# A hybrid encoder layer: the weight block sums of its FFN pairs on VectorE, and the norm factor behind one more unit

## The chip, the cores and the metric

The kernel runs on one core of a Trainium2 chip. Measured is the device time of one execution in microseconds (us); several runs are made, and their median is given. Engines are named as in the profile: PE is TensorE's matmul, PEld its weight load, DVE is VectorE, ACT is ScalarE, POOL is GpSimd, SP is the engine whose queue issues most DMAs.

## The reference

One layer of an encoder over 512 tokens of width 1024. Around every sub-layer stands an RMS norm; the first and the last sub-layer are SwiGLU feed-forward networks of width 2816, and between them stands a mixer of a recurrent branch and windowed attention.

```python
def swiglu(x, w1, w3, w2):
    return (jax.nn.silu(x @ w1) * (x @ w3)) @ w2

f = swiglu(rms_norm(h, ffn1_pre_g), ffn1_w1, ffn1_w3, ffn1_w2)
h = h + 0.5 * rms_norm(f, ffn1_post_g)
...                                   # recurrent branch and attention, merged by gates
f = swiglu(rms_norm(h, ffn2_pre_g), ffn2_w1, ffn2_w3, ffn2_w2)
h = h + 0.5 * rms_norm(f, ffn2_post_g)
```

Attention adds a bias looked up in a table of 32 buckets by 16 heads (`rel_bias`). All arrays are float32.

## The kernel before, in words

Every product is made from float32 operands that are split into a high part in fp32r and the remainder in fp32r: `hi` by an ACT copy, `lo` by a DVE subtraction (`split2`, lines 180 to 183; for weights `split_to`, lines 140 to 150). A product takes three matmuls: hi by hi, lo by hi, hi by lo.

A *unit* (`unit`, `mm_feat`, lines 185 to 202) makes one block of 128 output features for all 512 tokens: 8 steps of k times three matmuls, 24 matmuls of 512 columns, from one weight block of 128x1024. `get` hands out the next weight block and lets the following ones be loaded (`dma_to`, on SP's queue) and split (`split_to`) a fixed number of blocks ahead. The order of all weight blocks stands in the list `order`. Instructions run on each engine in the order in which the program emits them; nothing is rearranged. Work that belongs to a unit but is to be emitted later is put into a list by `later(n, fn)`, and `point()`, called twice in every unit and once in every product of a pair, emits what is due.

The first FFN begins with x in place of its norm: the norm's factor is one number a token, so it may be applied to the products. Three units (w1a 0, w3a 0, w1a 1) run as the loads arrive, then unit w3a 1 (line 643). Meanwhile ACT sums the squares of x (line 638), `rstd_of` makes the factor `r` (lines 215 to 230), and line 642 puts `r` on the diagonal of four 128x128 blocks (`dgs`). A float32 matmul of a block of ones with each of them (line 655) spreads the factor over all partitions; ACT copies it to `Rb`. In front of that a float32 matmul of the one-hot table with `rel_bias` (line 646) makes the row of biases for each head, which POOL's DMA queue writes out 128 times (`bias_scr`, 3 MB) for attention to read later. Then the first units are scaled with `Rb` and put through SiLU (`silu_mul`), x itself is scaled (`norm_x`, line 722) and cut into quarters for the pairs, while the units 2 to 5 of w1a and w3a run (`swiglu_units`).

The other blocks of the two FFNs are made in *pairs* (`class Pairs`): two weight blocks of one matrix, taken as a 2x2 matrix of blocks with the activations as another, are multiplied with seven products in place of eight, by sums of blocks. There are 16 such jobs in the first FFN and 18 in the second, w1 and w3 by turns. A product (`mm_s`) has 12 matmuls of 256 columns. `prep(m, i)` gets job m's weights ready:

- step 0 makes the four weight sums `S12` and `S34` on POOL (lines 478 to 481),
- steps 1 to 4 split the raw block, `S12`, `S34` and the block `a22`.

While job n runs, steps 1 to 4 of job n + 1 are emitted, at its end step 0 of job n + 2, and then the loads for job n + 3. In job n the order on PE is: a11, s1, then a22 of the job before (`last`), s2, a12, s4, s3; in the very last job a12 comes behind s3. The partial results are taken out of PSUM by ACT copies (`q1`, `q5`, `u`, `v`, lines 510 to 537) and DVE adds (lines 528, 533, 538). The bank `bu` holds a11, then a11 + s2, then s3 on top, then a22 on top: each product that is added must wait until the sum so far has been read. `tail` (`w2_ahead`) splits the first two hidden blocks and the first two blocks of w2 in the last job, for the product that follows (`tok_gemm`).

All tiles share 38 slots of 4 KB a partition, and all PSUM tiles 8 banks; a tile waits until the one that had its slot before has been read for the last time.

Of the kernel before, what the change touches and what calls it, by code (L numbers as in the profile page):

```python
# [15 lines left out]
P = 128  # L16
# [35 lines left out]
def hybrid_layer(ctx: ExitStack, tc: tile.TileContext, a: dict, out: bass.AP):  # L52
# [10 lines left out]
    def slot(shape, dt=F32, name="s"):  # L63
        uid[0] += 1
        return sb.tile(shape, dt, tag="slot", name=f"{name}_{uid[0]}")

    def bank(name="ps"):
        uid[0] += 1
        return pp.tile([P, 512], F32, tag="ps", name=f"{name}_{uid[0]}")
# [96 lines left out]
    def later(n, fn, rank=1):  # L166
        uid[0] += 1
        due.append((now[0] + n, rank, uid[0], fn))
# [29 lines left out]
    def unit(nm, i, **kw):  # L198
        w = get(nm, i)
        ps = bank("f")  # L200
        mm_feat(ps, w, **kw)
        return ps
# [185 lines left out]
    def silu_mul(ps1, ps3, R=None):  # L388

        t = slot([P, 2, SEQ], name="sw")  # L390
        if R is None:
            act.activation(t[:, 0, :], ps1, AF.Silu)
            dve.tensor_tensor(out=t[:, 1, :], in0=ps3, in1=t[:, 0, :], op=ALU.mult)
        else:
            dve.tensor_tensor(out=t[:, 0, :], in0=ps1, in1=R, op=ALU.mult)
            dve.tensor_tensor(out=t[:, 1, :], in0=ps3, in1=R, op=ALU.mult)
            act.activation(t[:, 0, :], t[:, 0, :], AF.Silu)
            dve.tensor_tensor(out=t[:, 1, :], in0=t[:, 1, :], in1=t[:, 0, :], op=ALU.mult)
        return t[:, 1, :]
# [40 lines left out]
    class Pairs:  # L440
# [13 lines left out]
        def prep(self, m, i):  # L454
            if m >= len(self.jobs):
                return
            k = self.k0 + 2 * m
            if i == 0:
                if k not in loaded or k + 1 not in loaded:
                    self.raws(m)  # L460
                s12, s34 = slot([P, 2 * QH], name="S12"), slot([P, 2 * QH], name="S34")
                self.w[m] = {"r": (raws.pop(k), raws.pop(k + 1)), "s": (s12, s34)}
            W = self.w[m]
            (ra, rb), (s12, s34) = W["r"], W["s"]
            a11, a12, a21, a22 = ra[:, :QH], ra[:, QH:], rb[:, :QH], rb[:, QH:]

            def both(src, w=2 * QH):
                hi = slot([P, w], F32R, name="whi")
                lo = slot([P, w], F32R, name="wlo")
                split2(hi, lo, src)  # L470
                return hi, lo

            def halves(p, a, b):
                W[a] = p[0][:, :QH], p[1][:, :QH]
                W[b] = p[0][:, QH:], p[1][:, QH:]

            if i == 0:
                pool.tensor_tensor(out=s12[:, :QH], in0=a21, in1=a22, op=ALU.add)
                pool.tensor_tensor(out=s12[:, QH:], in0=s12[:, :QH], in1=a11, op=ALU.subtract)
                pool.tensor_tensor(out=s34[:, QH:], in0=a12, in1=s12[:, QH:], op=ALU.subtract)  # L480
                pool.tensor_tensor(out=s34[:, :QH], in0=a11, in1=a21, op=ALU.subtract)
            elif i == 1:
                halves(both(ra), "a11", "a12")
            elif i == 2:
                halves(both(s12), "s1", "s2")
            elif i == 3:
                halves(both(s34), "s3", "s4")
            elif i == 4:
                t = slot([P, 2, QH], F32R, name="w22")
                split2(t[:, 0, :], t[:, 1, :], a22)  # L490
                W["a22"] = t[:, 0, :], t[:, 1, :]
                del W["r"], W["s"]

        def run(self, tail, hooks={}):
            X = self.X
            assert st["get"] == st["split"] == self.k0, (st, self.k0)
            st["get"] = st["split"] = self.k0 + 2 * len(self.jobs)
            last = lambda: None
            for n, (nm, f) in enumerate(self.jobs):
                W = self.w.pop(n)  # L500
                first = nm == self.na
                tmp = slot([P, 4, 256], name="ct")
                q1, q5, u, v = (tmp[:, i, :] for i in range(4))
                c = slot([P, 2, SEQ], name="cc")
                if first:
                    self.c1[f] = c
                bu, bx, bc = (bank("c")[:, :256] for _ in range(3))
                at = lambda i: [f() for f in hooks.get((n, i), ())]
                mm_s(W["a11"], X["b11"], bu)
                act.activation(q1, bu, AF.Copy)  # L510
                at(1)
                mm_s(W["s1"], X["t1"], bx)
                act.activation(q5, bx, AF.Copy)
                at(2)
                last()
                self.prep(n + 1, 1)
                mm_s(W["s2"], X["t2"], bu, True)
                del W["s1"], W["s2"]
                act.activation(u, bu, AF.Copy)
                at(3)  # L520
                if n == len(self.jobs) - 1:
                    tail()
                self.prep(n + 1, 2)

                def c11():
                    mm_s(W["a12"], X["b21"], bc)
                    del W["a11"], W["a12"]
                    dve.tensor_tensor(out=c[:, 0, :256], in0=bc, in1=q1, op=ALU.add)

                if n < len(self.jobs) - 1:  # L530
                    c11()
                mm_s(W["s4"], X["b22"], bx, True)
                dve.tensor_tensor(out=c[:, 0, 256:], in0=bx, in1=u, op=ALU.add)
                self.prep(n + 1, 3)
                mm_s(W["s3"], X["t3"], bu, True)
                del W["s3"], W["s4"]
                act.activation(v, bu, AF.Copy)
                dve.tensor_tensor(out=c[:, 1, 256:], in0=v, in1=q5, op=ALU.add)
                if n == len(self.jobs) - 1:
                    c11()  # L540
                if first:
                    act.activation(c[:, 0, :], c[:, 0, :], AF.Silu)
                    act.activation(c[:, 1, 256:], c[:, 1, 256:], AF.Silu)
                else:
                    c1 = self.c1[f]
                    dve.tensor_tensor(out=c1[:, 0, :], in0=c1[:, 0, :], in1=c[:, 0, :], op=ALU.mult)
                    dve.tensor_tensor(out=c1[:, 1, 256:], in0=c1[:, 1, 256:], in1=c[:, 1, 256:], op=ALU.mult)
                self.prep(n + 1, 4)
                self.prep(n + 2, 0)
                self.raws(n + 3)  # L550

                def last(W=W, bu=bu, c=c, f=f, first=first):
                    mm_s(W.pop("a22"), X["t4"], bu, True)
                    if first:
                        act.activation(c[:, 1, :256], bu, AF.Silu)
                    else:
                        c1 = self.c1.pop(f)
                        dve.tensor_tensor(out=c1[:, 1, :256], in0=bu, in1=c1[:, 1, :256], op=ALU.mult)
                        self.hid.f += [c1[:, 0, :], c1[:, 1, :]]

            last()
# [40 lines left out]
    dma_one(pairs_a.k0)  # L602
    dma_one(pairs_a.k0 + 1)
    make_identity(nc, ident)
    ones = slot([P, P], name="ones")
    pool.memset(ones, 1.0)
    oh = slot([N_BUCKETS, NREL + 1 + N_HEADS], name="oh")
    pool.dma_start(out=oh[:, : NREL + 1], in_=a["onehot"])
    pool.dma_start(out=oh[:, NREL + 1 :], in_=a["rel_bias"])
    ps = [bank("f") for _ in range(NS)]  # L610

    def split_first(u, kp):
# [24 lines left out]
        junk = slot([P, D], name="junk")  # L637
        act.activation(junk, h_all[:, t, :], AF.Square, accum_out=s4[:, t : t + 1])
    r = rstd_of(s4)
    dgs = slot([P, NT, P], name="dgs")  # L640
    for t in range(NT):
        dve.tensor_scalar(out=dgs[:, t, :], in0=ident, scalar1=r[:, t : t + 1], scalar2=None, op0=ALU.mult)
    ps.append(unit("w3a", 1))

    pse = bank("e")
    pe.matmul(pse[:N_HEADS, : NREL + 1], oh[:, NREL + 1 :], oh[:, : NREL + 1], start=True, stop=True)
    erow = slot([N_HEADS, NREL + 1], name="erow")
    act.activation(erow, pse[:N_HEADS, : NREL + 1], AF.Copy)
    scr = tc.dram_tile([N_HEADS, P, NREL], F32, name="bias_scr")
# [1 line left out]
    pool.dma_start(out=scr, in_=bass.AP(tensor=ev.tensor, offset=ev.offset, ap=[ev.ap[0], [0, P], ev.ap[1]]))  # L651
    Rb = slot([P, SEQ], name="Rb")
    psr = bank("r")
    for t in range(NT):
        pe.matmul(psr[:, t * P : (t + 1) * P], ones, dgs[:, t, :], start=True, stop=True)
    act.activation(Rb, psr, AF.Copy)
    pairs_a.prep(0, 1)
    pairs_a.prep(0, 2)
# [23 lines left out]
        dve.tensor_scalar(out=cneg, in0=z[3], scalar1=-4.0, scalar2=None, op0=ALU.mult)  # L682
        dve.tensor_scalar(out=bhalf, in0=vec[:, V_BA : V_BG + 16], scalar1=0.5, scalar2=None, op0=ALU.mult)

    def swiglu_units(na, nb, f0, f1, hid, R=None):
        for f in range(f0, f1):
            p1, p3 = unit(na, f), unit(nb, f)
            later(1, lambda p1=p1, p3=p3: hid.f.append(silu_mul(p1, p3, R)))

    def uview(hh, th):  # L690

# [40 lines left out]
    later(11, lambda: X1.update(t2=to_slots(tn[1])))  # L732
    end = 2 * 2 * (NC1 - 2)
    later(end - 1, lambda: pairs_a.prep(1, 0))
    swiglu_units("w1a", "w3a", 2, NC1, hid, Rb)
    point(True)
    X1["b21"] = to_uT(xn[1, 0], 1, 0)

# [441 lines left out]
```

## Time and profile before

| | us |
|---|---|
| median of 3 runs | 1155.74 |
| lowest, highest | 1155.67, 1157.07 |
| span of the profiled execution, first to last instruction | 1155.6 |
| PE busy in that span | 1138.0 |
| DVE busy | 779.9 |
| ACT busy | 574.3 |
| POOL busy | 353.0 |

The profile shows one execution of its own. Its page gives the span alone as the execution's time; the runs are timed from outside. A row of a timeline reads: start and length in us, engine, line of the kernel, operation, output and inputs, their shapes, how many were merged, and in brackets how long the engine had been idle before and what ended that. The second number in the row of a group is the mean in ns of one. Matmul rows overlap, since matmuls are pipelined: what counts there is the distance from start to start.

### The profile page before, as it was taken

What the parts mean: (1) busy time and instruction counts of PE and PEld (TensorE: products, weight loads), DVE (VectorE), ACT (ScalarE), POOL (GpSimd) and SP (SyncE); (2) the same over time, 40 slices, a digit from 0 to 9 for tenths busy, and PEclk for the clock granted to TensorE, in tenths of its full rate; (3) what the DMA queues carried; (4) which work ended last, traced back from release to release, by engine and by line L of the source; (5) the groups of instructions that cost most, each with busy time, mean ns of one, the idle gap of its engine ahead of it and who ended that gap; (6) DMA issues with size and microseconds to landing.
All of it is one profiled execution on the core that took longest, in us unless ns stands there. A gap on an engine that the chain in (4) does not pass through costs nothing.

```text
span 1155.6 us, 17108 instructions
## 1 busy us (share of the span) xinstructions
PE 1138.0 (98%) x6691; PEld 1011.8 (88%) x6691; DVE 779.9 (67%) x1195; ACT 574.3 (50%) x1020; POOL 353.0 (31%) x263
## 2 busy tenths in 40 slices
PE   9999999999999999999999999999999999999997
PEld 7788999988888888888888788888899999998886
DVE  5887788876337755685668764667868688885313
ACT  6444555574324457844646553255645545564211
POOL 1137777600001000001546550000646667700000
PEclk9999999999999999999999899999999999999999
DMA  9942332264313121234132223342133223254101
GB/s 343 148 125 80 110 110 94 83 207 158 116 37 128 55 66 63 74 111 127 56 92 74 81 69 124 109 146 74 37 110 110 82 102 111 92 183 168 51 19 54
DMA packets 35649, 120.73 MB, mean 104 GB/s; under 512 B 4273, under 2 KB 5809, under 8 KB 35569
## 3 DMA queue, kind: packets, MB, share of 16 engines
q1 hardware_dynamic: 32976, 110.95, 29.1%
q0 software_dynamic: 2448, 8.43, 4.0%
q8 instruction: 52, 0.85, 0.3%
q10 hardware_dynamic: 144, 0.26, 0.1%
q14 instruction: 29, 0.23, 0.1%
HBM read 114.40 MB, written 5.23 MB: 104 GB/s over the span
## 4 chain that ended last, share of the span: by engine, by line
PE 86%; DVE 6%; ACT 3%; DMA 2%; issue 1%; POOL 1%; SPq 0%; DVEq 0%; POOLq 0%; ACTq 0%
PE f L194 10%; PE f L193 10%; PE f L192 10%; PE c L435 10%; PE c L437 10%; PE c L436 10%; PE acc L212 8%; PE acc L210 8%; PE acc L211 8%; POOL P L981 1%; DMA h_all<-in_x_dram 1%; DMA xt<-in_xT_dram 1%; DVE wlo L183 1%; PE pt L997 1%; DVE P L966 1%
## 5 line engine op out<-in xcount | busy, mean ns | idle before, releaser
L192 PE MATMUL f<-uT,whi 128*128 128x512 f32 (+1 forms) x536 | 197.4, 368 | 0.5 <-ACT uT L289 0.5
L193 PE MATMUL f<-uT,wlo 128*128 128x512 f32 (+1 forms) x536 | 196.2, 366 | 0.6 <-DVE wlo L148 0.6
L194 PE MATMUL f<-uT,whi 128*128 128x512 f32 (+1 forms) x536 | 196.0, 366 | 0.4 <-DVE uT L290 0.4
L210 PE MATMUL acc<-whi,hT 128*128 128x512 f32 x352 | 137.3, 390 | 0.0
L211 PE MATMUL acc<-wlo,hT 128*128 128x512 f32 x352 | 137.2, 390 | 0.0
L212 PE MATMUL acc<-whi,hT 128*128 128x512 f32 x352 | 137.1, 389 | 0.0
L436 PE MATMUL c<-Xh,wlo 128*128 128x256 f32 x408 | 115.7, 284 | 2.0 <-DVE wlo L183 2.0
L183 DVE TENSOR_TENSOR wlo<-S,whi 128x1024 fp32r<-128x1024 f32 x68 | 111.7, 1643 | 7.9 <-ACT whi L182 7.8
L193 PEld LDWEIGHTS f<-uT,wlo 128*128 128x128 f32 x536 | 101.7, 190 | 17.0 <-DVE wlo L148 1.3
L435 PE MATMUL c<-Xh,whi 128*128 128x256 f32 x408 | 115.8, 284 | 0.8 <-ACT ct L510 0.8
L194 PEld LDWEIGHTS f<-uT,whi 128*128 128x128 f32 x536 | 101.5, 189 | 17.1 <-DVE uT L290 0.9
L192 PEld LDWEIGHTS f<-uT,whi 128*128 128x128 f32 x536 | 101.7, 190 | 16.7 <-ACT uT L289 1.0
L436 PE MATMUL c<-uT,wlo 128*128 128x256 f32 x408 | 115.7, 284 | 0.0
L437 PE MATMUL c<-Xl,whi 128*128 128x256 f32 x408 | 115.7, 283 | 0.0
L435 PE MATMUL c<-uT,whi 128*128 128x256 f32 x408 | 115.7, 283 | 0.0
L437 PE MATMUL c<-uT,whi 128*128 128x256 f32 x408 | 115.7, 283 | 0.0
L436 PEld LDWEIGHTS c<-Xh,wlo 128*128 128x128 f32 x408 | 78.4, 192 | 2.3 <-DVE wlo L183 2.2
L981 POOL TENSOR_SCALAR P<-P,d 128x256 f32<-128x256 f32 (+1 forms) x64 | 63.2, 1003 | 53.2 <-DVE d L979 37.0
L435 PEld LDWEIGHTS c<-Xh,whi 128*128 128x128 f32 x408 | 78.4, 192 | 1.0 <-ACT ct L510 1.0
L436 PEld LDWEIGHTS c<-uT,wlo 128*128 128x128 f32 x408 | 78.4, 192 | 0.0
L435 PEld LDWEIGHTS c<-uT,whi 128*128 128x128 f32 x408 | 78.4, 192 | 0.0
L437 PEld LDWEIGHTS c<-uT,whi 128*128 128x128 f32 x408 | 78.4, 192 | 0.0
(307 smaller groups left out, 2695.4 us busy)
## 6 DMA issues: line engine op xcount, KB each, us to landing
raw_w2a<-in_w2a_dram SPq DMA_DIRECT2D x22, 512.0 KB, 4.2
raw_w1b<-in_w1b_dram SPq DMA_DIRECT2D x22, 512.0 KB, 4.3
raw_w3b<-in_w3b_dram SPq DMA_DIRECT2D x22, 512.0 KB, 4.1
raw_w2b<-in_w2b_dram SPq DMA_DIRECT2D x22, 512.0 KB, 4.0
raw_w3a<-in_w3a_dram SPq DMA_DIRECT2D x21, 512.0 KB, 4.3
raw_w1a<-in_w1a_dram SPq DMA_DIRECT2D x20, 512.0 KB, 4.2
raw_wg<-in_wg_dram SPq DMA_DIRECT2D x16, 512.0 KB, 3.6
raw_xr<-in_xr_dram SPq DMA_DIRECT2D x8, 512.0 KB, 3.7
```

The source lines that it names most:

```text
L183: dve.tensor_tensor(out=lo, in0=src, in1=f32(hi), op=ALU.subtract)
L192: pe.matmul(ps[:, c0:c1], wh[:, s], h_, start=k == 0, stop=False)
L193: pe.matmul(ps[:, c0:c1], wl[:, s], h_, start=False, stop=False)
L194: pe.matmul(ps[:, c0:c1], wh[:, s], l_, start=False, stop=k == KT - 1)
L210: pe.matmul(acc[n], x[:, 0, c], wh[:, s], start=first, stop=False)
L211: pe.matmul(acc[n], x[:, 0, c], wl[:, s], start=False, stop=False)
L212: pe.matmul(acc[n], x[:, 1, c], wh[:, s], start=False, stop=last)
L435: pe.matmul(ps, wh[:, s], xh, start=first, stop=False, skip_group_check=True)
L436: pe.matmul(ps, wl[:, s], xh, start=False, stop=False, skip_group_check=True)
L437: pe.matmul(ps, wh[:, s], xl, start=False, stop=k == 3, skip_group_check=True)
L966: dve.tensor_tensor_reduce(out=pt[:, x, b0:256], in0=pss[x // 2][:, (x % 2) * 256 : (x % 2) * 256 + n], in1=BT[g][:, x, b0:256], scale=1.0 ...
L981: pool.tensor_scalar(out=pt[:, x, b0:256], in0=pt[:, x, b0:256], scalar1=d[:, x : x + 1], scalar2=None, op0=ALU.mult)
```

## The change

- The four weight sums of `prep` step 0 go from POOL to DVE, at the same place in the program.
- The copy `v` of the bank `bu` is left out; the add that used it (line 538) reads the bank itself.
- In the last job of a run of pairs `tail` is called behind the first product in place of behind s2.
- The factor's diagonal blocks are split into high and low parts (ACT, then DVE) in fp32r, and so is the bias table; the one-hot table is copied to fp32r. The spread becomes two matmuls of 512 columns in place of eight passes over 128 columns, the table two matmuls of 384 columns with 128 rows of weights.
- Between unit w3a 1 and these matmuls unit w1a 2 is emitted (`p1`), and `swiglu_units` takes it over in place of making it.

```diff
             if i == 0:
-                pool.tensor_tensor(out=s12[:, :QH], in0=a21, in1=a22, op=ALU.add)
-                pool.tensor_tensor(out=s12[:, QH:], in0=s12[:, :QH], in1=a11, op=ALU.subtract)
-                pool.tensor_tensor(out=s34[:, QH:], in0=a12, in1=s12[:, QH:], op=ALU.subtract)
-                pool.tensor_tensor(out=s34[:, :QH], in0=a11, in1=a21, op=ALU.subtract)
+                dve.tensor_tensor(out=s12[:, :QH], in0=a21, in1=a22, op=ALU.add)
+                dve.tensor_tensor(out=s12[:, QH:], in0=s12[:, :QH], in1=a11, op=ALU.subtract)
+                dve.tensor_tensor(out=s34[:, QH:], in0=a12, in1=s12[:, QH:], op=ALU.subtract)
+                dve.tensor_tensor(out=s34[:, :QH], in0=a11, in1=a21, op=ALU.subtract)
...
                 mm_s(W["a11"], X["b11"], bu)
                 act.activation(q1, bu, AF.Copy)
+                if n == len(self.jobs) - 1:
+                    tail()
                 at(1)
...
                 at(3)
-                if n == len(self.jobs) - 1:
-                    tail()
                 self.prep(n + 1, 2)
...
                 mm_s(W["s3"], X["t3"], bu, True)
                 del W["s3"], W["s4"]
-                act.activation(v, bu, AF.Copy)
-                dve.tensor_tensor(out=c[:, 1, 256:], in0=v, in1=q5, op=ALU.add)
+                dve.tensor_tensor(out=c[:, 1, 256:], in0=bu, in1=q5, op=ALU.add)
...
-    ones = slot([P, P], name="ones")
-    pool.memset(ones, 1.0)
+    ones = slot([P, P], F32R, name="ones")
+    pool.memset(f32(ones), 1.0)
...
+    ohr = slot([N_BUCKETS, NREL + 1], F32R, name="ohr")
+    rb = slot([N_BUCKETS, 2, P], F32R, name="rb")
+    pool.memset(f32(rb), 0.0)
...
-    dgs = slot([P, NT, P], name="dgs")
+    dgs = slot([P, 2, NT, P], F32R, name="dgs")
     for t in range(NT):
-        dve.tensor_scalar(out=dgs[:, t, :], in0=ident, scalar1=r[:, t : t + 1], scalar2=None, op0=ALU.mult)
+        act.activation(dgs[:, 0, t, :], ident, AF.Copy, scale=r[:, t : t + 1])
+    for t in range(NT):
+        dve.scalar_tensor_tensor(out=dgs[:, 1, t, :], in0=ident, scalar=r[:, t : t + 1], in1=f32(dgs[:, 0, t, :]), op0=ALU.mult, op1=ALU.subtract)
+    act.activation(ohr, oh[:, : NREL + 1], AF.Copy)
+    split2(rb[:, 0, :N_HEADS], rb[:, 1, :N_HEADS], oh[:, NREL + 1 :])
     ps.append(unit("w3a", 1))
+    p1 = unit("w1a", 2)
...
-    pe.matmul(pse[:N_HEADS, : NREL + 1], oh[:, NREL + 1 :], oh[:, : NREL + 1], start=True, stop=True)
+    for e in range(2):
+        pe.matmul(pse[:, : NREL + 1], rb[:, e, :], ohr, start=e == 0, stop=e == 1)
...
-    for t in range(NT):
-        pe.matmul(psr[:, t * P : (t + 1) * P], ones, dgs[:, t, :], start=True, stop=True)
+    for e in range(2):
+        pe.matmul(psr, ones, dgs[:, e, :, :].rearrange("p a b -> p (a b)"), start=e == 0, stop=e == 1)
...
         for f in range(f0, f1):
-            p1, p3 = unit(na, f), unit(nb, f)
+            p1, p3 = p1 or unit(na, f), unit(nb, f)
             later(1, lambda p1=p1, p3=p3: hid.f.append(silu_mul(p1, p3, R)))
+            p1 = None
```

More of the change, by code (lines that the diff above doesn't have):

```diff
@@ L502, in run @@
                 tmp = slot([P, 4, 256], name="ct")
-                q1, q5, u, v = (tmp[:, i, :] for i in range(4))
+                q1, q5, u = (tmp[:, i, :] for i in range(3))
                 c = slot([P, 2, SEQ], name="cc")
@@ L683, in softplus, with swiglu_units @@
         dve.tensor_scalar(out=bhalf, in0=vec[:, V_BA : V_BG + 16], scalar1=0.5, scalar2=None, op0=ALU.mult)
-    def swiglu_units(na, nb, f0, f1, hid, R=None):
+    def swiglu_units(na, nb, f0, f1, hid, R=None, p1=None):
         for f in range(f0, f1):
-            p1, p3 = unit(na, f), unit(nb, f)
+            p1, p3 = p1 or unit(na, f), unit(nb, f)
             later(1, lambda p1=p1, p3=p3: hid.f.append(silu_mul(p1, p3, R)))
+            p1 = None
     def uview(hh, th):
@@ L734, in hybrid_layer @@
     later(end - 1, lambda: pairs_a.prep(1, 0))
-    swiglu_units("w1a", "w3a", 2, NC1, hid, Rb)
+    swiglu_units("w1a", "w3a", 2, NC1, hid, Rb, p1)
     point(True)
```

## The prediction

> **What bounds the kernel now.** I read the page's head first, then who TensorE (PE) waited for, then the windows around those waits, and last the timelines of the engines there.
>
> ```profile
> span 1155.6 us, 17108 instructions
> PE 1138.0 (98%) x6691; PEld 1011.8 (88%) x6691; DVE 779.9 (67%) x1195; ACT 574.3 (50%) x1020; POOL 353.0 (31%) x263
> ```
>
> PE is busy for 98% of the span. The change removes hardly any matmul work, so only PE's 17.6 us of idle time, and slow matmuls, can be won. The profiled span, 1155.6 us, stands 0.1 us from the median of the runs, 1155.74; I add the sum to the median. A measurement of this kernel can tell about 0.2% (2.3 us) from no change.
>
> ```profile
> PE s L960 <- DVE QS L910: 2.4, 1, 2.4
> PE c L436 <- DVE wlo L183: 2.0, 1, 2.0
> PE r L655 <- DVE dgs L642: 1.7, 2, 1.0
> PE c L435 <- ACT ct L510: 0.8, 1, 0.8
> PE f L193 <- DVE wlo L148: 0.6, 1, 0.6
> ```
>
> Columns are us in total, times, longest. Rows 2 to 5 lie where the diff works: at the norm factor (near 30 us) and where the first pair jobs begin (near 90 us). Row 1 is attention, untouched.
>
> ```profile
> 28.30:32.60 4.30, 2.63 (x11) 1.64 (x11) 4.16 (x7) 0.48 (x1) 3.72 (x4) 0.86 0.85 342
> 32.60:35.00 2.40, 2.40 (x8) 1.94 (x8) 0.54 (x2) 1.99 (x3) 0.00 (x0) 0.54 0.93 111
> 130.63:150.79 20.16, 20.16 (x171) 20.16 (x169) 16.52 (x19) 10.89 (x19) 14.15 (x8) 1.00 0.32 98
> 640.00:660.00 20.00, 17.46 (x77) 14.74 (x75) 16.50 (x43) 14.21 (x41) 12.01 (x12) 0.83 0.27 80
> ```
>
> Columns: length; busy PE, PEld, DVE, ACT, POOL; granted clock. Behind the wait at 30 us the clock was granted at 0.54, so the wait was paid twice. The third row is two steady pair jobs: PE has no idle time there, and DVE has 3.6 us left of 20.16.
>
> **Part 1: norm factor and bias table behind one more unit.**
>
> ```profile
> 28.00 0.39 PE L194 MATMUL f<-uT,whi 128*128 128x512 f32 x1
> 28.32 0.82 PE L646 MATMUL e<-oh 32*16 32x384 f32 x2
> 31.26 1.72 PE L655 MATMUL r<-dgs,ones 128*128 128x128 f32 x6 [0.67 <-DVE dgs L642]
> 32.63 0.78 PE L192 MATMUL f<-uT,whi 128*128 128x512 f32 x1
> 35.12 0.39 PE L192 MATMUL f<-uT,whi 128*128 128x512 f32 x1
> 44.66 0.39 PE L192 MATMUL f<-uT,whi 128*128 128x512 f32 x1
> 45.60 0.50 PE L193 MATMUL f<-uT,wlo 128*128 128x512 f32 x1 [0.55 <-DVE wlo L148]
> ```
>
> From 35.12 to 44.66 run 42 matmuls: 0.227 us each, 5.45 a unit of 24. The unit before ends at 28.00 + 0.23 = 28.23. By 35.12 six matmuls of the next are done (1.36), so table, factor, waits and low clock cost PE 35.12 - 28.23 - 1.36 = 5.5 us. Afterwards they are four fp32r matmuls of at most 512 columns. No row has them behind a full PE; at 0.227 they cost 0.9, and between half of that and the spacing under the low clock ((35.12 - 32.63) / 6 = 0.42) 0.5 to 1.7. I take 0.9, the row of the same shape: 4.6 us won, if the operands are there when the extra unit ends, at 28.23 + 5.45 = 33.7.
>
> ```profile
> 25.88 1.29 POOL L478 TENSOR_TENSOR S<-raw_w1a 128x512 f32<-128x512 f32 x1 [23.16 <-DMA raw_w1a<-in_w1a_dram]
> 24.21 0.17 DVE L219 TENSOR_SCALAR v<-s 128x4 f32<-128x4 f32 x1 [3.86 <-ACT junk L638]
> 25.94 1.25 DVE L226 TENSOR_TENSOR e<-r 128x4 f32<-128x4 f32 x1
> 28.88 3.25 DVE L642 TENSOR_SCALAR dgs<-ident,r 128x128 f32<-128x128 f32 x4
> 33.01 0.60 ACT L656 ACTIVATE Rb<-r 128x512 f32<-128x512 f32 x1 [3.37 <-PE r L655]
> 40.19 0.68 DVE L395 TENSOR_TENSOR sw<-f,Rb 128x512 f32<-128x512 f32 x1
> 40.79 0.68 DVE L396 TENSOR_TENSOR sw<-f,Rb 128x512 f32<-128x512 f32 x1
> 44.33 1.22 DVE L148 TENSOR_TENSOR wlo<-raw_w1a,whi 128x1024 fp32r<-128x1024 f32 x1
> ```
>
> The first weight sums now stand ahead of `v` in DVE's queue and wait for the raw weights until 25.88. Four adds at 0.60 (40.79 - 40.19) to 0.68 make 28.5; `v` starts there, not at 24.21. Behind it five tiny steps and ScalarE's root take about 1.4: the 1.25 us for 128x4 overlaps a POOL add, as `dgs` at 3.25 does, and POOL is now quiet. So the factor stands near 30.0. Its high parts are four ACT copies of 128 columns, which no row has: more than nothing, less than the 0.60 of the 512-column `Rb`; I take 0.25, and as much for the low parts, which follow on DVE one behind the other. That is 31.3, and near 31.7 with the table's parts; at 0.60 each it would be 33.0, still under the extra unit. On SP the same raw loads go out in the same order, only earlier in the program, so nothing is moved past them; two more small tiles are taken from slots long free.
>
> Part of this is given back. Rb came at 33.01 and comes at 33.7 + 0.9 + 0.15 = 34.75, 1.75 later, and all that ACT and DVE do behind it (first split pair, two SiLUs, S34, w22) moves too. Before, the next weight split in DVE's queue (44.33, done at 45.55) was what PE waited for at 45.60, at unit w1a 3. That unit's split is now ahead of Rb, and the same place belongs to w3a 3: done near 47.3. PE reaches its first low-part matmul at 33.7 + 0.9 + 10.9 + 0.2 = 45.7 and loses 1.6. Before, that matmul would have run at 45.60 + 5.45 = 51.05. The gain there is 51.05 - 47.3 = 3.7 us.
>
> **Part 2: weight sums on DVE, first pair jobs.**
>
> ```profile
> 78.54 0.69 DVE L396 TENSOR_TENSOR sw<-f,Rb 128x512 f32<-128x512 f32 x1 [3.70 <-PE f L194]
> 78.34 0.28 PE L435 MATMUL c<-Xh,whi 128*128 128x256 f32 x1
> 81.40 1.22 DVE L183 TENSOR_TENSOR uT<-xn,uT 128x1024 fp32r<-128x1024 f32 x1 [0.23 <-ACT uT L182]
> 83.92 2.32 DVE L183 TENSOR_TENSOR wlo<-raw_w3a,whi 128x1024 fp32r<-128x1024 f32 x1
> 86.17 2.31 DVE L183 TENSOR_TENSOR uT<-T,uT 128x1024 fp32r<-128x1024 f32 x1
> 88.40 2.28 DVE L183 TENSOR_TENSOR wlo<-S,whi 128x1024 fp32r<-128x1024 f32 x1
> 83.39 1.77 POOL L478 TENSOR_TENSOR S<-raw_w1a 128x512 f32<-128x512 f32 x1 [7.99 <-DMA raw_w1a<-in_w1a_dram]
> 90.74 0.39 PE L436 MATMUL c<-Xh,wlo 128*128 128x256 f32 x1 [2.04 <-DVE wlo L183]
> ```
>
> The same subtraction takes 1.22 with POOL quiet and 2.3 from the moment POOL's adds begin. Three such rows (83.92, 86.17, 88.40) lie ahead of the stall at 90.74: 3.2 us too long against a stall of 2.04. Without POOL this chain ends 1 us before PE needs it; the 0.8 us wait for `ct` was the echo of the late `wlo` (ScalarE queued behind it). Both go: 2.8 us. In return the sums of job 1 (2.6) come on DVE just before the jobs, ahead of the last SiLU of the single units and of the first `uT` parts. DVE idled 3.7 us there before (78.54), so they hide in that idle time. If it shrinks, because PE arrives 3.7 us earlier and DVE doesn't, the first products wait: the `uT` of 81.40 was done 4.3 us behind the jobs' start (78.34) and is read by the fifth product, 48 matmuls of 0.12 (20.16 / 168) or 5.8 us behind it, which leaves 1.5 us.
>
> **Part 3: the 34 pair jobs.**
>
> ```profile
> L183 DVE TENSOR_TENSOR wlo<-S,whi 128x1024 fp32r<-128x1024 f32 x27 | 46.8, 1734 | 3.7 <-ACT whi L182 3.6
> L538 DVE TENSOR_TENSOR cc<-ct 128x256 f32<-128x256 f32 x14 | 15.7, 1120 | 0.3 <-ACT ct L537 0.3
> L546 DVE TENSOR_TENSOR cc<-cc,cc 128x512 f32<-128x512 f32 x7 | 9.2, 1308 | 0.0
> L533 DVE TENSOR_TENSOR cc<-c,ct 128x256 f32<-128x256 f32 x14 | 5.8, 412 | 0.0
> ```
>
> These groups are DVE from 100 to 240 us, 14 jobs. DVE gains 4 x 0.60 = 2.4 us a job. It loses what POOL cost it: 27 x (1.73 - 1.22) + 14 x (1.12 - 0.41) + 7 x (1.31 - 0.68) = 28 us, 2.0 a job. L538 now reads PSUM as L533 does (0.41) and saves ScalarE a copy. Net +0.4: 17.3 of 20.16 us for two jobs. Cost on PE: nothing, while the order holds. The sums stand last in a job's DVE work, behind w22; what queues behind them is the next job's `wlo`, needed 2 us later or more. Their slots and raw tiles were free earlier (POOL ran ahead of them). The final product of a block must wait for L538 to read its bank; two products of 1.44 us lie between. Without that cover it costs the length of the DVE operation ahead, about 1.2 us a job. In the very last job one product (1.44) lies between, and the tail's two hT and two w2 splits (about 3.6 us of DVE at 0.60 and 1.22), which stood before that add, now run two products and more earlier, beside matmuls, when DVE has no sums left to make: 0. The price if their inputs are late is the wait of `q5` behind them on ACT, at most those 3.6 us, twice.
>
> [...]
>
> **Sum.** 3.7 + 2.8 = 6.5, less 0.3 for a low part of unit w1a 5 that I see coming just as PE needs it (POOL's one remaining sum still slows DVE's three beside it): 1155.7 - 6.2 = 1149.5. Its own range is 1147.5 to 1151.5.
>
> **Rivals.**
>
> *DVE becomes the bound (slower).* If the relief does not come, two jobs need 16.5 + 8 x 0.60 = 21.3 us of DVE in 20.16 us. From 20.16 on, each pair of jobs is longer by the excess: 17 x 1.1 = 19, less the 3.7 of the start: 1171. Against it: 1.22 against 2.3 above. Chance 0.06.
>
> *The pair start does not gain.* What decides are the raw weights of job 1:
>
> ```profile
> bias_scr<-erow POOLq DMA_DIRECT2D x1, 3064.0 KB, 33.3
> 68.14 1.94 POOL L478 TENSOR_TENSOR S<-raw_w3a 128x512 f32<-128x512 f32 x1 [11.42 <-DMA raw_w3a<-in_w3a_dram]
> ```
>
> The table's 3 MB transfer starts some 4 us later, and job 1's raw weights landed behind it, at 68.1. DVE now waits for them in order; at 4 us later they land near 72, when DVE gets there. Two or three us later still, and the stalls come back: 1155.7 - 3.7 = 1152. Chance 0.14.
>
> *The clock.* At 640 to 660 the grant of 0.83 means 6.8 us at half speed behind a 2.4 us wait: 3.4 us lost. A shift of the kernel, or my 1.6 us wait at 45.7, can add or drop a stretch of about 3.4 us at half speed, 1.7 us: 1151 to 1153, or 1148. Chance 0.13 for the worse. [...]
>
> *The cover fails.* If the factor isn't ready at 33.7, PE waits and cools as before; only part 2 remains: 1153. Chance 0.05.
>
> **Numbers.** Forecast 0.62. Faster by over 0.2% (under 1153.4): forecast, nearly all of the pair rival, most of the clock's and some of the cover's: 0.85. Within 0.2%: 0.07. Slower: 0.08, DVE and what I didn't see. The range takes in the rivals at 1152 and 1153; downwards no wait at 45.7 (1.6) and a better clock (1.7): 1146 to 1153.5.
>
> **What would show it.** Right: after the extra unit four short matmuls without idle time and no half clock before 40 us; `wlo` at 1.22 throughout the jobs; DVE 17.3 us in two jobs; a PE wait for `wlo` near 46 us of 1 to 2 us; none at 90. Wrong: PE waits for `wlo` or `cc` in every job, or DVE waiting for raw weights before the first job.

## The result, and the profile after

| | before | after |
|---|---|---|
| device time, median (us) | 1156.4 | 1150.1 |
| lowest, highest | 1155.67, 1157.83 | 1149.83, 1150.53 |
| profiled execution: span | 1155.6 | 1147.9 |
| PE busy | 1138.0 | 1134.0 |
| DVE busy | 779.9 | 781.7 |
| POOL busy | 353.0 | 104.3 |

The ratio of the changed kernel to the one before, in runs side by side (four of each), is 0.9941, with a 95% interval of 0.9927 to 0.9955. The forecast was 1149.5 us. A run's time is longer than its span, in the profiled run of the changed kernel by 2.4 us (1150.3 and 1147.9): below, spans are compared with spans and times with times. The page's head and the list of who PE waited for (us in total, times, longest) after the change:

```profile
span 1147.9 us, 16879 instructions
PE 1134.0 (99%) x6685; PEld 1007.8 (88%) x6685; DVE 781.7 (68%) x1332; ACT 567.7 (49%) x992; POOL 104.3 (9%) x128
```

```profile
PE s L969 <- DVE QS L919: 2.3, 1, 2.3
PE w L584 <- DVE warm L581: 1.5, 1, 1.5
PE f L193 <- DVE wlo L148: 1.2, 2, 0.9
...
PE c L435 <- ACT ct L510: 0.2, 1, 0.2
```

The waits for `dgs` (1.7 us) and for the pairs' `wlo` (2.0) are gone, the one for `ct` is down from 0.8 to 0.2. What is left near the edits is the third row: low parts of two single units. DVE is no busier than before, although it makes 136 sums that POOL made. The same four windows as before (length; busy PE, PEld, DVE, ACT, POOL; granted clock; DMA share; GB/s):

```profile
28.30:32.60 4.30, 4.30 (x21) 3.56 (x20) 3.17 (x13) 2.22 (x8) 0.00 (x0) 1.00 0.92 375
32.60:35.00 2.40, 2.40 (x11) 1.60 (x10) 1.63 (x2) 1.95 (x3) 0.00 (x0) 1.00 0.04 17
130.63:150.79 20.16, 20.16 (x170) 20.16 (x169) 16.91 (x25) 10.47 (x17) 0.00 (x0) 1.00 0.35 105
640.00:660.00 20.00, 17.31 (x86) 14.81 (x85) 15.88 (x50) 12.74 (x39) 11.82 (x15) 0.91 0.26 79
```

At 28 to 35 us PE is full and its clock is whole. Two steady pair jobs hold 16.91 us of DVE work in 20.16. The last window is attention, which the change does not touch: its granted clock rose from 0.83 to 0.91.

Where in the execution the time was won shows in the start of each stage on PE (the first matmul of that kind, in the profiled executions; the last two columns are two executions of the changed kernel against the one before):

| stage | before | after | shift | shift, second execution |
|---|---|---|---|---|
| first pair product | 78.34 | 75.04 | -3.30 | -3.53 |
| product with w2, after 16 jobs | 242.95 | 237.07 | -5.88 | -6.09 |
| attention | 545.93 | 540.06 | -5.87 | -6.08 |
| product after attention | 754.22 | 746.66 | -7.56 | -7.25 |
| second FFN's pairs | 847.27 | 839.67 | -7.60 | -7.29 |
| last matmul | 1148.18 | 1140.58 | -7.60 | -7.29 |

So 3.3 us come from the start, 2.6 from the first FFN's pairs, nothing from the second FFN's 18 jobs, and 1.2 to 1.7 from attention. There the grant is 0.50 for 6.80 us in the execution before, and for 3.40 in the one after:

```profile
649.20:656.00 6.80, 6.08 (x20) 5.24 (x21) 5.67 (x18) 5.21 (x18) 4.82 (x5) 0.50 0.26 74
```

```profile
643.80:647.20 3.40, 3.04 (x13) 2.88 (x14) 2.36 (x9) 2.73 (x7) 2.47 (x2) 0.50 0.02 5
```

Matmuls of 512 columns start 0.43 us apart within the first of them (653.64 and 654.07) and 0.23 ahead of it (642.06 and 642.29), so 3.4 us less of it are worth about 1.6 us of PE's time. That part belongs to the clock, not to an edit.

### The profile page after: what moved, and what is told of

Read it like the earlier page. It is cut to its first block, busy times and chain, and to the rows that moved or that the text cites. A ratio compares the mean times of both kernels' runs of the same rounds, so it can differ in the third digit from the quotient of the medians.

```text
span 1147.9 us, 16879 instructions
## 1 busy us (share of the span) xinstructions
PE 1134.0 (99%) x6685; PEld 1007.8 (88%) x6685; DVE 781.7 (68%) x1332; ACT 567.7 (49%) x992; POOL 104.3 (9%) x128
## 4 chain that ended last, share of the span: by engine, by line
PE 40%; DVE 6%; ACT 4%; POOL 1%; issue 1%; DMA 0%; DVEq 0%; POOLq 0%; ACTq 0%
PE c L437 5%; PE c L436 5%; PE c L435 5%; PE acc L211 4%; PE acc L212 4%; PE acc L210 4%; PE f L194 4%; PE f L192 3%; PE f L193 3%; ACT P L983 2%; DVE P L975 1%; ACT whi L147 1%; POOL P L990 1%; DVE wlo L148 1%; PE pt L1006 0%
## 5 line engine op out<-in xcount | busy, mean ns | idle before, releaser
L194 PEld LDWEIGHTS f<-uT,whi 128*128 128x128 f32 x536 | 101.1, 189 | 16.9 <-DVE uT L290 0.9
L183 DVE TENSOR_TENSOR wlo<-S,whi 128x1024 fp32r<-128x1024 f32 x68 | 82.9, 1220 | 18.0 <-ACT whi L182 18.0
L437 PEld LDWEIGHTS c<-Xl,whi 128*128 128x128 f32 x408 | 78.3, 192 | 0.0
```

Of the source, the lines that this page charges most:

```text
L183: dve.tensor_tensor(out=lo, in0=src, in1=f32(hi), op=ALU.subtract)
L194: pe.matmul(ps[:, c0:c1], wh[:, s], l_, start=False, stop=k == KT - 1)
L437: pe.matmul(ps, wh[:, s], xl, start=False, stop=k == 3, skip_group_check=True)
```

## The experiments

Each time stands against runs of the kernel before beside it, whose medians lay between 1156.96 and 1157.24 us in these comparisons.

**The changed kernel again**, the base for the rest.

> The kernel after, unchanged, beside the others on the same chip: 1150.1 and a ratio to before of 0.994. If the two parts add up, its gain is that of the two kernels with one part each together, 6 us; if they overlap it is less than their sum.

1150.33 us, 0.9943 [0.9928, 0.9958].

**Sums alone.** The kernel before, with `prep` step 0 on DVE and nothing else:

```diff
-                pool.tensor_tensor(out=s12[:, :QH], in0=a21, in1=a22, op=ALU.add)
+                dve.tensor_tensor(out=s12[:, :QH], in0=a21, in1=a22, op=ALU.add)
...
```

> The kernel before with only the four weight sums on VectorE. Theory (two separate gains, start of the kernel and first pair jobs): the waits near 90 us (2.0 and 0.8 us) go, so the jobs of the first FFN reach the next stage 2.7 us earlier; the start is as before within 0.5 us, since the factor's chain begins 2.5 us later behind the sums but runs without POOL's adds beside it. 1156.4 - 2.7 = 1153.7. Rival (the sums cost VectorE more than they free, and only the extra unit hides it): the start is 1 to 2 us later and the sum is about 1155 to 1156. Rival (the sums alone make all of the gain): 1150.

1151.42 us, 0.9953 [0.9939, 0.9967]: 2.3 us better than expected. The timeline of the start, with the only wait of PE that is left where the change works:

```profile
30.33 0.87 DVE L642 TENSOR_SCALAR dgs<-ident,r 128x128 f32<-128x128 f32 x4
30.76 1.13 PE L655 MATMUL r<-dgs,ones 128*128 128x128 f32 x8 [1.50 <-DVE dgs L642]
```

With POOL quiet the four `dgs` blocks take 0.87 us in place of 3.25, so the move also shortened the start: the pairs begin 1.1 us earlier. Both waits at the first jobs are gone, and the 16 jobs take 161.27 us, the bare 16 x 84 x 0.12. That is 3.3 us less than before, not 2.8. In its profiled execution attention is 1.6 us shorter as well, by the clock (0.91 from 640 to 660 us).

**Start alone.** The changed kernel with sums on POOL, with ScalarE's copy `v`, and with `tail` behind s2.

> The kernel after with the weight sums back on POOL, the copy v and the late tail: only the start is changed. Theory: the start gains 3 to 4 us (three matmul groups at full clock behind the extra unit, no wait for the factor), the waits of 2 to 3 us in the first pair jobs remain: 1156.4 - 3.4 = 1153.0. Rival (the two parts need each other: with POOL's adds beside it the factor's chain is not done when the extra unit ends): no gain at the start, 1155 to 1156.

1153.6 us, 0.9970 [0.9961, 0.9979]. The pairs begin 3.9 us earlier, and then:

```profile
84.81 2.28 DVE L183 TENSOR_TENSOR wlo<-S,whi 128x1024 fp32r<-128x1024 f32 x1
87.14 0.39 PE L436 MATMUL c<-Xh,wlo 128*128 128x256 f32 x1 [2.35 <-DVE wlo L183]
```

The stall that the sums caused is there, behind a subtraction of 2.28 us. In this execution a stretch at half clock follows it (0.91 from 80 to 100 us), and the pairs give 0.8 us back. The two parts alone add up to about 8.9 us by their ratios (0.47% and 0.30% of 1157) and give 6.6 together. At least 1.1 us of that is won twice: a quiet POOL shortens the same chain at the start that the extra unit covers. The other 1.2 us lie within the intervals.

**The extra unit without the fp32r parts.** The kernel before, with only `p1` moved ahead of the table and the spread:

```diff
     ps.append(unit("w3a", 1))
+    p1 = unit("w1a", 2)
...
```

> The kernel before with one edit: the first pair unit of the FFN (w1a 2) stands ahead of the matmuls of e and r, which stay in fp32; sums by GpSimd, ScalarE's copy of v and the late tail as before. Theory (the one more unit is what takes PE's waits near 28 to 32 us away; the fp32r parts only shorten PE's own work by about 1.1 us): most of what the start alone gave, 1154.5 us (1153.8 to 1155.3). Rival A (the fp32r parts carry the gain): no gain, 1157. Rival B (without the high and low parts VectorE and ScalarE are less loaded, so the unit alone is as good as both): 1153.6 or less.

1155.9 us, 0.9994 [0.9983, 1.0005]: no difference that can be told, where 1153.8 to 1155.3 was expected. In its profile the pairs begin 1.9 us earlier than before, 2.0 later than with both halves of the start. The timeline of PE, and that of ACT:

```profile
33.23 0.39 PE L194 MATMUL f<-uT,whi 128*128 128x512 f32 x1
33.55 0.81 PE L647 MATMUL e<-oh 32*16 32x384 f32 x2
34.29 1.16 PE L656 MATMUL r<-dgs,ones 128*128 128x128 f32 x8
35.21 0.48 PE L192 MATMUL f<-uT,whi 128*128 128x512 f32 x1
46.61 0.49 PE L192 MATMUL f<-uT,whi 128*128 128x512 f32 x1 [0.25 <-ACT whi L147]
48.14 0.50 PE L193 MATMUL f<-uT,wlo 128*128 128x512 f32 x1 [1.04 <-DVE wlo L148]
```

```profile
40.16 1.28 ACT L397 ACT_TABLE_LOAD   x1 [2.12 <-DVE sw L395]
41.46 0.63 ACT L397 ACTIVATE sw<-sw 128x512 f32<-128x512 f32 x1
```

The cover does its work: no wait before `e` and `r`. The float32 passes cost PE 35.21 - 33.23 - 0.23 = 1.75 us, 0.6 more than the fp32r matmuls. The other loss comes later, two waits of together 1.29 us at w3a 3, where the changed kernel has 0.23. ScalarE's table load for SiLU waits here for VectorE's product (`sw`), so 1.28 us of load stand between that product and SiLU. In the changed kernel the load runs before:

```profile
37.91 1.28 ACT L397 ACT_TABLE_LOAD   x1
39.25 0.68 DVE L395 TENSOR_TENSOR sw<-f,Rb 128x512 f32<-128x512 f32 x1
39.97 0.63 ACT L397 ACTIVATE sw<-sw 128x512 f32<-128x512 f32 x1 [0.78 <-DVE sw L395]
```

Added to the cover's 1.9 us, these two losses of 0.6 and 1.1 make 3.6 of the 3.9 us that both halves gain together. Part of the gain is also lost later: behind the first jobs' wait for `wlo` the profiled execution has a stretch at half clock (0.91 from 80 to 100 us), which the kernel before does not have there (1.00).

**The fp32r parts without the extra unit.**

```diff
-    p1 = unit("w1a", 2)
+    p1 = None
```

(in the kernel "start alone", so that w1a 2 is made in its old place)

> The changed start without the one more unit: e and r from fp32r high and low parts directly behind the statistics' sums, w1a 2 in its old place; sums by GpSimd, ScalarE's copy of v and the late tail as before. Theory (PE waits out the chain of VectorE and ScalarE, which the low parts make no shorter, and the clock drops behind it as before): nothing or little gained, 1156.5 us (1155.5 to 1157.5). Rival A (fewer passes over PE are the gain): 1154 or less. Rival B (the longer chain of parts costs more than the passes save): 1158 or more.

1157.59 us, 1.0007 [0.9997, 1.0017]: nothing gained. The timeline and a window:

```profile
30.67 0.44 PE L655 MATMUL e<-ohr,rb 32*128 32x384 f32 x1 [2.79 <-ACT rb L182]
31.94 0.68 PE L655 MATMUL e<-ohr,rb 32*128 32x384 f32 x1 [0.84 <-DVE rb L183]
```

```profile
32.60:35.00 2.40, 2.40 (x7) 1.92 (x7) 0.42 (x1) 1.61 (x3) 1.03 (x1) 0.50 0.37 85
```

PE waits 3.63 us for the chain of parts, and behind it the clock is granted at 0.50. Neither half of the start is worth anything measurable alone; together they give 3.5 us.

**The table load taken off the chain.** To test the reading of the load, the kernel with the extra unit alone got one tiny SiLU ahead of the first real one:

```diff
     pairs_a.prep(0, 2)
+    act.activation(small(1, "tl"), vec[:, 0:1], AF.Silu)
     hid.f += [silu_mul(ps[0], ps[1], Rb), silu_mul(ps[2], ps[3], Rb)]
```

> The kernel cover_only (one more unit ahead of e and r, both left in fp32) with one tiny SiLU of 128x1 on ScalarE put behind the first pair's weight parts, ahead of the first real SiLU, so that ScalarE's table load runs while it is idle instead of behind its wait for VectorE. Theory (the load of 1.28 us behind that wait is what makes the low part of w3a 3 late in cover_only, where PE waits 1.04 us at 48.1 and 0.25 at 46.6; the changed kernel escapes it because its load does not wait): the first SiLU starts within 0.1 us of VectorE's product, the wait at 48 goes to under 0.3, the pairs start 1.0 to 1.3 us earlier than in cover_only (76.46 to about 75.3), and the time is 1 us lower, 1154.8 (1154.0 to 1155.3). Rival (the load is not what the low part waits for, the order of VectorE's queue is): wait and time as in cover_only, 1155.9.

1155.21 us, 0.9984 [0.9975, 0.9993]. ScalarE's and VectorE's timelines:

```profile
38.38 1.28 ACT L660 ACT_TABLE_LOAD   x1
39.67 0.20 ACT L660 ACTIVATE tl<-vec 128x1 f32<-128x1 f32 x1
39.72 0.68 DVE L395 TENSOR_TENSOR sw<-f,Rb 128x512 f32<-128x512 f32 x1
40.50 0.63 ACT L397 ACTIVATE sw<-sw 128x512 f32<-128x512 f32 x1 [0.62 <-DVE sw L395]
```

SiLU now starts 0.1 us behind VectorE's product, PE's wait at w3a 3 is 0.28 in place of 1.29, and the pairs begin at 75.45 in place of 76.46. The pairs come 1.0 us earlier, as much as the wait is shorter: the load's place was the cause. The run times moved the same way (0.9994 to 0.9984), though their intervals overlap; in the two profiled spans (1152.8 both) the gain is lost again in attention.

**The last sum of the tokens on DVE.** The third row of PE's waits after the change holds 0.94 us at unit w1a 5. Its timeline:

```profile
57.17 1.22 DVE L710 TENSOR_TENSOR T<-xn,xn 128x1024 f32<-128x1024 f32 x1
57.40 3.23 POOL L709 TENSOR_TENSOR T<-xn,xn 128x1024 f32<-128x1024 f32 x1 [20.86 <-DVE xn L731]
58.42 3.30 DVE L711 TENSOR_TENSOR T<-xn,T 128x1024 f32<-128x1024 f32 x1
```

The ends are what to look at: POOL's row ends at 60.63, 2.24 us behind the end of DVE's first (58.39), and DVE's second ends at 61.72, 1.09 behind POOL's. In the second FFN the same sum on POOL ends at 810.20 (2.42 us), and DVE's row beside it, a weight subtraction begun at 808.67, ends at 811.27 (2.60 us in place of 1.22), 1.07 behind it. That fits two instructions of which one stands until the other is through, and not two that slow each other a little; it is read from these ends alone, and no run tests it by itself. The one sum left on POOL costs DVE 2.1 us (3.30 in place of 1.22) and would cost 1.2 on DVE itself:

```diff
-        pool.tensor_tensor(out=t[2], in0=xf[1, 1], in1=xf[0, 1], op=ALU.subtract)
+        dve.tensor_tensor(out=t[2], in0=xf[1, 1], in1=xf[0, 1], op=ALU.subtract)
```

> The kernel after with the one sum of activations that POOL still makes (line 709) on VectorE too, in both FFNs. Theory: the 3.3 us row of the sum beside it falls to 1.2, VectorE is about 1 us earlier at the split of unit w1a 5, and PE's wait of 0.9 us there goes: 1150.1 - 0.9 = 1149.2. Rival (VectorE is late there by its own load): nothing gained, 1150.1, or 0.3 lost.

1148.89 us, 0.9930 [0.9915, 0.9946]. PE's wait there is 0.16 us, and the pairs begin 0.8 to 1.0 us earlier than in the two executions of the changed kernel. The interval of the ratio overlaps that of the changed kernel: the gain is shown in the trace, not yet in the time.

**Half the sums made twice.** From job 2 on the last two of the four sums are made a second time, to use up DVE's slack.

> The kernel after with two of a job's four weight sums made twice on VectorE (the same values again, jobs 2 and later). Theory (VectorE has room in the pair jobs; PE sets their pace): 16.9 us of VectorE in two jobs become 16.9 + 4 x 0.65 = 19.5, below 20.16: no change, 1150.3 within 0.5. Rival (VectorE is already late at single steps of a job, and only the average has room): each job is longer by the added 1.3 us or a part of it, 1160 to 1190.

1150.21 us, 0.9942 [0.9928, 0.9957], as expected: in the steady jobs 2.1 us more DVE work in two jobs cost PE nothing. The window of two jobs, and the one new wait of PE:

```profile
130.63:150.79 20.16, 20.16 (x170) 20.16 (x169) 19.02 (x30) 10.47 (x18) 0.00 (x0) 1.00 0.33 105
```

```profile
232.07 0.38 PE L435 MATMUL c<-uT,whi 128*128 128x256 f32 x1 [0.79 <-ACT ct L518]
```

That wait lies in the last job of the first FFN, where ScalarE's copy `q5` stands behind the tail's splits. The time does not show it: in the profiled execution attention has no half clock (1.00 from 640 to 660 us), which gives most of it back.

**All sums made twice.**

> The kernel after with all four weight sums made twice on VectorE (the same values again, jobs 2 and later, 30 jobs). Theory: 16.9 + 8 x 0.65 = 22.1 us of VectorE in two jobs of 20.16 us: VectorE sets the pace, 1.0 us more a job, 1150.3 + 30 = 1180. This is the slow rival of the prediction, provoked. Rival (there is more room than the busy time says): 1150 to 1155.

1192.4 us, 1.0304 [1.0284, 1.0324]. A window of 40 us within the jobs, and the two leading rows of PE's waits:

```profile
160.00:200.00 40.00, 36.62 (x293) 35.20 (x292) 38.51 (x60) 17.64 (x27) 0.00 (x0) 1.00 0.30 97
```

```profile
PE c L436 <- DVE wlo L183: 18.3, 28, 0.7
PE c L435 <- DVE cc L542: 7.3, 29, 0.3
```

19.0 us in 20.16 are free, 22.4 (16.9 and 8 x 0.69) are not. DVE then is the bound and PE waits in nearly every job. The 30 jobs with doubled sums cost 42 us, 1.4 each, so two jobs last 23.0 us. DVE is busy for 38.5 of 40 us, or 22.1 of these 23.0, and nearly all of the rest is one wait of 1.0 us for a high part from ScalarE (eight of them in the 16 jobs of the first FFN). The expected 1180 had counted DVE's busy time alone: (22.1 - 20.16) / 2 = 1.0 a job.

**The tail back behind s2.**

> The kernel after with the tail's splits back behind s2 in the last job. Theory: the add that now reads PSUM stands behind them on VectorE, ends about 1.4 us after the last product could begin, and that product must wait for it: one wait of 1 to 1.5 us in each FFN, 1150.3 + 2.6 = 1152.9. Rival (the tail's place is free, as it was before): 1150.3.

1152.95 us, 0.9961 [0.9947, 0.9975]. The last job of the first FFN, in VectorE's and PE's timeline, and the row of PE's waits:

```profile
234.69 1.22 DVE L148 TENSOR_TENSOR wlo<-raw_w2a,whi 128x1024 fp32r<-128x1024 f32 x1
236.16 0.41 DVE L537 TENSOR_TENSOR cc<-c,ct 128x256 f32<-128x256 f32 x1
236.63 0.39 PE L435 MATMUL c<-uT,w 128*128 128x256 f32 x1 [1.29 <-DVE cc L537]
```

```profile
PE c L435 <- DVE cc L537: 2.6, 2, 1.3
```

The add that reads PSUM itself stands behind the tail's splits, and a22 of the last job may not touch the bank before it: 1.29 us in each FFN, 2.6 together, which is the difference in time. Once the bank is read directly, the earlier tail pays for itself.

**ScalarE's copy put back** (`v` copied, then added, as before).

> The kernel after with the ScalarE copy v back between PSUM and the add. Theory: the pair jobs are PE's, so the copy (0.38 us of ScalarE a job) costs nothing: 1150.3 within 0.5. Rival (the read of PSUM itself saves time in every job): 0.1 to 0.3 us a job, 1153 to 1160.

1150.75 us, 0.9945 [0.9933, 0.9958]: no difference. The groups from 100 to 240 us (mean in ns, then idle time before):

```profile
L538 DVE TENSOR_TENSOR cc<-ct 128x256 f32<-128x256 f32 x14 | 6.0, 426 | 5.3 <-ACT ct L537 5.3
```

and the same add in the changed kernel:

```profile
L537 DVE TENSOR_TENSOR cc<-c,ct 128x256 f32<-128x256 f32 x14 | 5.9, 419 | 0.9 <-PE c L437 0.9
```

The add takes 0.42 us from either memory. Its 1.12 of before was POOL's doing.

**A version that beats both.** The largest wait left was attention's 2.3 us for `QS`, whose low part DVE makes behind four scores. On top of the token sum on DVE, a finished q block's parts go first:

```diff
-            later(1, lambda i=i, ps=ps: q_out(i, ps))
+            later(1, lambda i=i, ps=ps: q_out(i, ps), -1)
```

> The kernel with the token sum on VectorE (token_sum_dve) and one edit in the attention: the parts of a finished q block are taken ahead of the scores that fall due at the same point, so VectorE subtracts QS's low part before it reads the scores. Theory (the wait of 2.3 us for QS's low part and the half clock that the trace shows 3.4 to 6.8 us long right behind it are lost time on PE's path, 1.7 to 3.4 us of it by the clock): 2 to 4 us less than token_sum_dve, 1146 us (1145 to 1147.2). Rival (the scores come about 2 us later by it, so their exponentials, transposes and the output behind them stall PE instead): no gain or up to 2 us lost, 1148.5 to 1151. A rival of its own: the wait goes but the half clock stays, since it comes from something other than the wait: 1147.

1147.62 us, 0.9922 [0.9906, 0.9938]. PE's wait for `QS` and the window in attention:

```profile
PE s L969 <- DVE QS L919: 1.0, 2, 0.7
```

```profile
640.00:660.00 20.00, 18.84 (x103) 15.99 (x103) 15.80 (x51) 12.03 (x38) 11.33 (x13) 1.00 0.24 77
```

The wait is down to 1.0 us in two parts and no half clock follows. In the profiles the product after attention starts 4.0 us earlier than with the token sum alone; in the medians 1.3 us are left, less than expected and with intervals that overlap, for the profiled execution without this edit had more half clock in attention than that of the changed kernel (0.83 against 0.91 from 640 to 660), and its six runs differ in the clock: three were granted 0.995, three 0.999.

## Why the prediction was right

The time came 0.6 us from the forecast, and each stage that the change touches gained what was forecast for it within 0.3 us. Three terms were off, and partly cancelled.

That the time itself came so close is in part luck. The forecast took its 6.2 us off 1155.7, while the kernel before had 1156.4 in the comparison and about 1157 in the later ones. The ratios make the gain 6.6 to 6.8 us, of which the edits give 5.9 to 6.1 by the stage table. That the profiled span lay 0.1 us from the median was a coincidence too: in its later runs that kernel's time is 1.8 us above its span (1157.04 and 1155.3), so the profiled execution was one of the slower ones.

**PE's cost of table and spread: 0.9 forecast, 1.2 measured.** The last matmul of unit w1a 2 is issued at 33.71 and the next unit's first at 35.13; without the former's own 0.23 that is 1.19 us:

```profile
33.71 0.39 PE L194 MATMUL f<-uT,whi 128*128 128x512 f32 x1
...
35.13 0.40 PE L192 MATMUL f<-uT,whi 128*128 128x512 f32 x1
```

**The operands in time: held, with less to spare than thought.** The table's last part was ready at 32.6, forecast 31.7, and the cover ends at 34.0:

```profile
26.43 0.69 DVE L478 TENSOR_TENSOR S<-raw_w1a 128x512 f32<-128x512 f32 x1 [5.20 <-DMA raw_w1a<-in_w1a_dram]
27.16 0.69 DVE L479 TENSOR_TENSOR S<-S,raw_w1a 128x512 f32<-128x512 f32 x1
...
32.42 0.16 DVE L183 TENSOR_TENSOR rb<-oh,rb 32x16 fp32r<-32x16 f32 x1 [0.17 <-ACT rb L182]
...
35.39 0.60 ACT L664 ACTIVATE Rb<-r 128x512 f32<-128x512 f32 x1 [0.18 <-PE r L663]
```

The first sum started 0.55 us later than in the execution before (26.43 against 25.88, when the raw weights landed), and a sum that needs the one ahead of it starts 0.73 us behind it, where the forecast had 0.60.

**What is given back: wrong in size.** `Rb` came at 35.39 (forecast 34.75), but the low part of w3a 3 was done at 46.6, not 47.3, and PE waited 0.23, not 1.6, so the sign that the prediction named, a wait of 1 to 2 us near 46, did not come. PE itself arrived at 46.42 rather than 45.7, which is the other half of the difference:

```profile
45.38 1.22 DVE L148 TENSOR_TENSOR wlo<-raw_w3a,whi 128x1024 fp32r<-128x1024 f32 x1
46.65 0.50 PE L193 MATMUL f<-uT,wlo 128*128 128x512 f32 x1 [0.23 <-DVE wlo L148]
```

The step that failed moved everything behind `Rb` by the same amount, ScalarE's table load with it. The semaphore instructions of SiLU's line, before and after:

```profile
L397 ACTq EVENT_SEMAPHORE  x4: 17/17/17, 37.6 to 74.9; - x4
```

```profile
L397 ACTq EVENT_SEMAPHORE  x2: 17/17/17, 42.0 to 51.5; - x2
```

Before, and in the kernels with the sums alone or one half of the start, the first of them stands at the load and holds it until `sw` is there. In the changed kernel the first comes with the second SiLU, at 42.0, and the load has run in ScalarE's idle time. The load's place is worth 1.3 us (the low part 0.7 earlier than forecast, behind an `Rb` 0.6 later); the preload experiment won 1.0 of them back. Why that first instruction is missing when both halves are there stays open.

**Unit w1a 5: 0.3 forecast, 0.94 measured.** The place and the cause were right. The size took three DVE rows as slowed a little; what the trace shows is one row longer by 2.1 us (3.30 in place of 1.22), and the rows on either side of it at 1.22 and 1.23. In the forecast's way of counting, the start gives 51.05 - 46.65 = 4.4 us at w3a 3, less 0.94 at w1a 5: 3.5, where 3.4 was forecast and the first pair product shows 3.3 and 3.5.

**The first pair jobs: 2.8 forecast, 2.6 measured.** The cause held in both directions: gone with the sums moved, there with the start alone. With the sums alone 3.3 us were won. The 0.7 between are two short pauses of PE in the first job, at 78.25 and 87.21 us, of the kind that the prediction named: PE comes earlier by the extra unit and DVE doesn't. At 78.25 PE waits for a ScalarE copy, which queued behind a SiLU that had waited 4.0 us for VectorE, busy with the sums of job 1. Of the rival with late raw weights nothing is to be seen; DVE made job 1's sums from 72.97 on without waiting.

**The 34 jobs: nothing forecast, nothing measured.** DVE's 16.91 us stand against 17.3 forecast, `wlo` at 1.22, L537 at 0.42. The slow rival's mechanism is real, as the doubled sums show, and needed more than another 2.1 us of DVE in two jobs to set in; with another 5.5 it had.

**The tail: right at 0**, and in the old place it costs 1.29 us, twice, by the DVE add. The price that the text named, `q5` behind late inputs on ScalarE, is real but was not due here: it shows where DVE is later, with 0.79 us once when half the sums are doubled and 1.3 us in each FFN when all are.

**The clock** moved the profiled gain from 5.9 to 7.6 us; the forecast kept it as a rival only, with the chance put mostly on the worse side. In the runs the changed kernel's granted clock lies between 0.996 and 0.999, that of the kernel before between 0.993 and 0.999, so part of the measured 0.6% is this. How much was not separated. Runs with the same grant differ by 6.3 us at 0.996 (means of 1157.0 and 1150.7) and by 4.7 at 0.998 (1155.0 and 1150.3), but the half clock at 30 us that the edit takes away (0.50 from 31.45 to 34.85 us in the execution before) counts in that grant too.

## What to carry to other kernels

Work moved onto a busier engine can be free if the engine that did it before was slowing that one down: count first what the two cost each other (here eight sums of 0.69 us, 5.5 together, came on in two jobs, and DVE's work there rose by 0.4, from 16.52 to 16.91 us). A covering unit and a shorter chain behind it may be worth nothing singly and much together (0.9994 and 1.0007 singly, 0.9970 together), so test such edits in pairs. Look where a table load stands relative to the wait of the instruction that needs it; a tiny early activation can take it off the chain (the load lasts 1.28 us, and PE's wait behind it went from 1.29 us to 0.28).

## What the runs showed that was not expected

- The length of a wait does not settle whether a half clock follows. One came behind waits of 1.50 us (the sums alone, at 30.76), 2.05 (the extra unit alone, at 88.87) and 2.3 to 2.4 (attention, in five executions: grants of 0.83 and 0.91 from 640 to 660 us). None came behind 2.04 us in the same place of the first jobs in the kernel before (1.00 from 80 to 100 us), nor behind attention's 2.3 in the run with half the sums doubled (1.00 from 640 to 660 us). The windows behind the first two of these waits:

```profile
31.80:35.20 3.40, 3.40 (x10) 2.63 (x10) 2.23 (x3) 2.49 (x3) 0.07 (x1) 0.50 0.79 105
88.90:92.40 3.50, 3.50 (x17) 3.50 (x18) 2.50 (x5) 1.63 (x4) 2.01 (x2) 0.51 0.00 0
```

  Stretches of 6.80 and of 3.40 us at a grant of 0.50 were seen in attention, behind waits of 2.41 and 2.31 us. What starts one, and how long it lasts, these runs do not show.
- A table load costs 1.28 us, and nothing more is seen around it: in the preload kernel the next activation starts at 39.67, 0.01 behind its end.
